# First modulation by column groups on TensorE, another last norm, and another instruction order up to the first FFN

## The chip, the core and the metric

One core of one Trainium2 chip runs the program, with its matrix engine (TensorE, PE in the profile), its vector engine (VectorE, DVE), its scalar engine (ScalarE, ACT), GpSimd (POOL) and SyncE (SP), which issues most DMAs. The metric is the device time of one execution, in microseconds, as the median over the runs.

## The reference

Two DeepNorm layers on a sequence of 512 positions of width 1024, all in float32. Each layer has a mixer and a SwiGLU channel mixer, and each of these four sublayers is modulated by the conditioning vector `c`:

```python
def ada_modulation(c, w, b):
    m = jax.nn.silu(c) @ w + b
    shift, scale, gate = jnp.split(m[:, None, :], 3, axis=-1)
    return shift, scale, gate

def residual_update(x, c, ada_w, ada_b, ln_g, ln_b, sublayer):
    shift, scale, gate = ada_modulation(c, ada_w, ada_b)
    out = sublayer(x * (1 + scale) + shift)
    return layer_norm(ALPHA * x + (1 + gate) * out, ln_g, ln_b)

def layer_norm(x, g, b):
    mu = jnp.mean(xf, axis=-1, keepdims=True)
    var = jnp.mean(jnp.square(xf - mu), axis=-1, keepdims=True)
    y = (xf - mu) * lax.rsqrt(var + LN_EPS)
    return y * g + b
```

`w` is 1024 x 3072 for each sublayer. Layer 0 mixes with sparse attention beside a chunked gMLP after one combined input projection; layer 1 with a short gated convolution. Nothing of `x * (1 + scale) + shift` can be multiplied by the first input projection before the first shift and scale are there.

## The kernel before

The 512 positions are four tiles of 128 rows (`t` = 0 to 3), the width eight chunks of 128 (`k` = 0 to 7). A float32 product is made of three products of rounded halves: high x high, high x low and low x high, each a matmul of 128 x 128 weights and 512 moving columns. So every weight is cast once (`hi`, ScalarE) and subtracted once (`lo`, VectorE or GpSimd), and every activation too.

*The start.* The chunks come in groups, `groups_k` = (0), (1), (2,3), (4,5), (6), (7). For each group SyncE loads, in this order, two slabs of modulation weights `aw` (shift and scale, `w` = 0 and 1; `group_load`, L777), the group's columns of `x` (`x_load`, L781) and the rows of three units of input weights (`unit_load`, L796). The modulation of a group is a sum over 1024 products: `ada_add` (L330, L332) multiplies each slab's column of eight by a scalar of silu(c) and adds on VectorE into `acs`, and `group_mms` (L824) adds over the partitions by a product with ones into `pq`. For slab (0, 0) alone (`ON_PE`) TensorE makes the whole sum, in eight products of one column. `group_sum` adds the bias. Then `x_turn` (L839) transposes the chunk into `px`, `x_affine` (L844) applies scale and shift into `v`, `x_high` (L850) casts it to `h`, `x_low` makes the low half, and `first_mms` (L861, L864) multiplies it with three units into six accumulators. ScalarE casts the weights of the units (`unit_high`, L803) in between. When the first unit's accumulators are complete, ScalarE copies them to `G` (L995), and the compression of keys (L1025, `pc`) reads `G`.

*Later modulations* are loaded as slabs `ar` and `ad` (L1099). Some are added on VectorE; others already by column groups on TensorE: `add` (L1108) puts 32 columns of `cz`, which are zero but for one column of silu(c), as weights into one of four column groups of the array, with 256 moving columns of the slab. `ad` has one buffer.

*The order.* `Plan` holds tasks, each with engines that it may run on, costs, dependencies and ring buffers. A plan isn't solved when the kernel is built: `Plan.follow` emits the tasks in the order of a table of numbers, `ORDER_0` and `ORDER_1`, where a number is four times the task's index plus the chosen engine. `ORDER_0` covers the start, `ORDER_1` everything from there up to the first four tiles of the first FFN. Each engine and each DMA queue does its work in the order of emission. Everything after that is written in program order, the same in both kernels but for the last norm.

*The end.* `tail_norm` (L1806) makes the last output product tile by tile; `Norm.rstd` and the function `newton` (L633) find 1/sqrt(var + eps) by an integer first guess and three Newton steps; `Norm.store` (L578) applies it. In the last norm (`s` = 3) the steps of tiles 0 to 2 run on ScalarE, nine small operations, then ScalarE scales (L585) and GpSimd multiplies and adds the rows of weights (L586, L587). For tile 3 VectorE does the steps and, in pieces of 512, 256 and 256 columns, the rest (L591, L593).

Of the kernel before, what the change touches and what calls it, by code (L numbers as in the profile page):

```python
# [7 lines left out]
F32 = mybir.dt.float32  # L8
# [214 lines left out]
def trunk(ctx: ExitStack, tc: tile.TileContext, x, c, ada_w, ada_b, ln_g, ln_b, even_w_in,  # L223
# [1582 lines left out]
    def tail_norm(acts, us, norm):  # L1806
# [3 lines left out]
        for t in range(ST):  # L1810
# [22 lines left out]
            if norm.s == 3:  # L1833
                norm.store(t, *pend)
# [195 lines left out]
```

## Time and profile before

| what | value |
|---|---|
| three runs | 1242.0, 1243.58 (median), 1244.14 us |
| the profiled execution | 1241.4 us, its span 1239.5 us |
| mean granted TensorE clock of it | 0.995 of full |
| busy: TensorE, VectorE, ScalarE, GpSimd | 1197.7, 781.1, 445.3, 137.4 us |

The span is what the profile covers of one execution; the 1.9 us between it and the execution's time lie around it. A timeline row has a start, a length, the operation with out and in by the program's names, and in brackets the idle time before and what ended it. Matmuls follow each other in a pipeline, so the step from one start to the next tells their rate better than their length does. The granted clock of 1.00 is 2.4 GHz.

### The profile page before, as it was taken

What the parts mean: (1) busy time and instruction counts of PE and PEld (TensorE: products, weight loads), DVE (VectorE), ACT (ScalarE), POOL (GpSimd) and SP (SyncE); (2) the same over time, 40 slices, a digit from 0 to 9 for tenths busy, and PEclk for the clock granted to TensorE, in tenths of its full rate; (3) what the DMA queues carried; (4) which work ended last, traced back from release to release, by engine and by line L of the source; (5) the groups of instructions that cost most, each with busy time, mean ns of one, the idle gap of its engine ahead of it and who ended that gap; (6) DMA issues with size and microseconds to landing.
All of it is one profiled execution on the core that took longest, in us unless ns stands there. A gap on an engine that the chain in (4) does not pass through costs nothing.

```text
span 1239.5 us, 15445 instructions
## 1 busy us (share of the span) xinstructions
PE 1197.7 (97%) x5939; PEld 981.9 (79%) x5939; DVE 781.1 (63%) x1306; ACT 445.3 (36%) x776; POOL 137.4 (11%) x235
## 2 busy tenths in 40 slices
PE   5899999998999999999999999999999999999996
PEld 4777777767988888888887988788988888888885
DVE  4775567886667675757766688456674353435346
ACT  2373258895423131212224422124423131313124
POOL 3130013475000000000002000002010000000005
PEclk9899999999999999999999999999999999999998
DMA  9784652131366455555630366330363232423301
GB/s 297 216 273 153 201 173 75 46 120 52 105 219 201 138 188 162 169 179 187 194 112 1 103 204 221 99 105 1 102 204 102 65 108 67 136 68 103 102 1 68
DMA packets 121465, 164.73 MB, mean 133 GB/s; under 512 B 5861, under 2 KB 87085, under 8 KB 121392
## 3 DMA queue, kind: packets, MB, share of 16 engines
q1 hardware_dynamic: 105552, 132.33, 34.0%
q10 hardware_dynamic: 14208, 26.75, 6.6%
q0 software_dynamic: 1632, 4.67, 1.3%
q8 instruction: 46, 0.75, 0.2%
q14 instruction: 27, 0.22, 0.1%
HBM read 161.63 MB, written 2.10 MB: 132 GB/s over the span
## 4 chain that ended last, share of the span: by engine, by line
PE 91%; DVE 3%; DMA 2%; ACT 2%; issue 1%; POOL 0%; SPq 0%; ACTq 0%; DVEq 0%
PE pi L524 51%; PE po L536 25%; PE pi L1269 5%; PE pi L861 1%; PE ph L1458 1%; DMA ar<-in_ada_w_dram 1%; PE po L1108 1%; PE ptp L1625 1%; PE pt L660 1%; PE pc L1025 1%; PE pi L864 1%; PE pvo L1639 1%; PE pvo L1640 1%; DMA ad<-in_ada_w_dram 0%; DMA aw<-in_ada_w_dram 0%
## 5 line engine op out<-in xcount | busy, mean ns | idle before, releaser
L524 PE MATMUL pi<-h,hi 128*128 128x512 f32 (+1 forms) x2016 | 576.0, 371 | 0.0
L524 PEld LDWEIGHTS pi<-h,hi 128*128 128x128 f32 x2016 | 365.2, 188 | 66.2 <-issue 1.4
L524 PE MATMUL pi<-h,lo 128*128 128x512 f32 (+1 forms) x1008 | 372.8, 370 | 0.0
L472 ACT ACTIVATE hi<-raw 128x1024 fp32r<-128x1024 f32 (+1 forms) x186 | 187.2, 1045 | 279.6 <-PE po L536 141.8
L476 DVE TENSOR_TENSOR lo<-raw,hi 128x1024 fp32r<-128x1024 f32 (+1 forms) x178 | 211.0, 1225 | 84.3 <-ACT hi L472 82.7
L524 PEld LDWEIGHTS pi<-h,lo 128*128 128x128 f32 x1008 | 189.7, 188 | 33.0
L541 DVE TENSOR_TENSOR xr<-xr,po 128x512 f32<-128x512 f32 x129 | 87.1, 681 | 128.5 <-PE po L536 128.3
L536 PE MATMUL po<-hi,ah 128*128 128x512 f32 (+1 forms) x420 | 165.8, 395 | 0.2
L536 PE MATMUL po<-hi,al 128*128 128x512 f32 (+1 forms) x420 | 164.5, 392 | 0.0
L536 PE MATMUL po<-lo,ah 128*128 128x512 f32 (+1 forms) x420 | 164.3, 391 | 0.0
L536 PEld LDWEIGHTS po<-hi,ah 128*128 128x128 f32 x420 | 79.0, 188 | 19.9 <-DVE xr L541 1.9
L536 PEld LDWEIGHTS po<-lo,ah 128*128 128x128 f32 x420 | 79.1, 188 | 17.7 <-issue 0.2
L536 PEld LDWEIGHTS po<-hi,al 128*128 128x128 f32 x420 | 79.0, 188 | 17.8
L1881 ACT ACTIVATE ah<-sg 128x512 fp32r<-128x512 f32 x44 | 27.8, 632 | 173.5 <-DVE sg L1926 173.5
L1926 DVE TENSOR_TENSOR sg<-sg,pi 128x512 f32<-128x512 f32 x44 | 30.2, 687 | 90.5 <-PE pi L524 90.3
L462 DVE TENSOR_TENSOR raw<-raw,gateb 128x1024 f32<-128x1024 f32 x60 | 70.9, 1219 | 4.1 <-DMA raw<-in_even_w_out_dram 4.1
L1922 ACT ACTIVATE sg<-pi 128x512 f32<-128x512 f32 x44 | 26.2, 595 | 117.3 <-PE pi L524 117.2
L332 DVE SCALAR_TENSOR_TENSOR acc<-ar,cs,acc 128x512 f32<-128x512 f32 x84 | 63.0, 750 | 3.3 <-DMA ar<-in_ada_w_dram 1.5
L1269 PE MATMUL pi<-hi,h 128*128 128x512 f32 (+1 forms) x192 | 59.8, 377 | 0.0
L1882 DVE TENSOR_TENSOR al<-sg,ah 128x512 fp32r<-128x512 f32 x44 | 30.5, 693 | 30.7 <-ACT ah L1881 30.7
L670 ACT ACTIVATE v<-pt,b,g 128x128 f32<-128x128 f32 x88 | 32.9, 454 | 44.0 <-PE pt L660 35.7
L637 POOL TENSOR_SCALAR v<-mv 128x1 f32<-128x1 f32 x10 | 2.5, 254 | 394.8 <-DVE mv L572 394.6
(255 smaller groups left out, 1250.3 us busy)
## 6 DMA issues: line engine op xcount, KB each, us to landing
raw<-in_ffn_w_in_dram SPq DMA_DIRECT2D x88, 512.0 KB, 4.6
ar<-in_ada_w_dram ACTq DMA_DIRECT2D x48, 512.0 KB, 4.3
raw<-in_ffn_w_out_dram SPq DMA_DIRECT2D x44, 512.0 KB, 4.3
ar<-in_ada_w_dram SPq DMA_DIRECT2D x24, 512.0 KB, 5.5
raw<-in_odd_w_in_dram SPq DMA_DIRECT2D x24, 512.0 KB, 4.6
raw<-in_even_w_in_dram SPq DMA_DIRECT2D x10, 512.0 KB, 5.3
aw<-in_ada_w_dram SPq DMA_DIRECT2D x8, 512.0 KB, 6.0
aw<-in_ada_w_dram SPq DMA_DIRECT2D x4, 1024.0 KB, 8.9
```

Of the source, the lines that this page charges most:

```text
L332: dve.scalar_tensor_tensor(acc, r, cs[:, k:k + 1], acc, op0=ALU.mult, op1=ALU.add)
L462: e.tensor_tensor(z[:, k, :], z[:, k, :], gateb[fold == 2], op=ALU.mult)
L472: act(hl[0][:, i * n0:i * n0 + n0], raw(i), AF.Copy)
L476: e.tensor_tensor(hl[1][:, sl], self.raw.pop(2 * u + i), hl[0][:, sl], op=ALU.subtract)
L524: mm(p[:, sl], w, h[z][k // 4][:, k % 4, sl], start=k == 0 and i == 0, stop=k == KT - 1 and i == 2)
L536: mm(p[:, c], s_, w[:, k % 2, c0], start=first and i == 0, stop=last and i == n - 1)
L541: dve.tensor_tensor(z, z, p[:, c], op=ALU.add)
L670: act(v[:, q, :], p[:, q, :], AF.Identity, scale=g1[s][:, k:k + 1], bias=b1[s][:, k:k + 1])
L1269: mm(tiles[t], s_, w[:, q, :], start=k == 0 and z == 0, stop=k == 7 and z == 2)
L1881: act(a[0][:, k, :], f, AF.Copy)
L1882: dve.tensor_tensor(a[1][:, k, :], f, a[0][:, k, :], op=ALU.subtract)
L1926: dve.tensor_tensor(f, f, p, op=ALU.mult)
```

## The change

*Start.* `ON_PE` now lists all six groups. `group_cols` makes, for each group and `w`, eight products with the four column groups (`tile_position`), with the same `cz` weights as the later modulations; `group_settle` copies the result `pg` to `acs` on ScalarE; `group_mms` adds over the partitions with ones, now always one product for a chunk. VectorE's `ada_add` isn't used for these groups.

```diff
-    def group_mms(g, w, on_pe):
+    def group_cols(g, w):
+
+        n = len(groups_k[g]) * P
+        if w == 0:
+            bx["pa", g] = ps.tile([P, 2, n], F32, name="pg", tag="tr")
+        for i in range(2):
+            for q in range(4):
+                k = 4 * i + q
+                mm(bx["pa", g][32 * q:32 * q + 32, w, :], cz[:, k // 2, k % 2:k % 2 + 32],
+                   bx["aw", g, w][:, k, :], start=i == 0, stop=i == 1,
+                   tile_position=(0, 32 * q))
+
+    def group_settle(g):
+        n = len(groups_k[g]) * P
+        bx["acc", g] = st.tile([P, 2, n], F32, name="acs", bufs=2)
+        act(bx["acc", g], bx["pa", g], AF.Copy)
+
+    def group_mms(g, w):
         n = len(groups_k[g])
         if ("pm", g) not in bx:
             bx["pm", g] = ps.tile([P, 2, n], F32, name="pq", tag="tr")
         for j in range(n):
-            sl = slice(j * P, j * P + P)
-            for k in range(KT) if on_pe else (0,):
-                mm(bx["pm", g][:, w, j:j + 1],
-                   bx["aw", g, w][:, k, sl] if on_pe else bx["acc", g][:, w, sl],
-                   cs[:, k:k + 1] if on_pe else ones[:, 0:1], start=k == 0,
-                   stop=not on_pe or k == KT - 1)
+            mm(bx["pm", g][:, w, j:j + 1], bx["acc", g][:, w, j * P:j * P + P], ones[:, 0:1],
+               start=True, stop=True)
...
-    ON_PE = ((0, 0),)
+    ON_PE = (0, 1, 2, 3, 4, 5)
...
+        if g in ON_PE:
+            got = []
+            for w in (0, 1):
+                got.append(plan.add(("pe", .1 + .28 * n, lambda g=g, w=w: group_cols(g, w)),
+                                    [aws[g][w][1], cz_t] + got[-1:], k0, acq=[] if w else ["tr"]))
+            head = last = plan.add(("act", .12 + .21 * n, lambda g=g: group_settle(g)), got, k0,
+                                   acq=["acc"], rel=[(got[0], "tr")])
```

*Planner.* The cost of an addition on TensorE is lower, and the Newton steps of the first layer's norms may run on GpSimd or VectorE.

```diff
-            last = plan.add(("pe", .5, lambda i=i: add(i)), [a, last], key,
+            last = plan.add(("pe", .3, lambda i=i: add(i)), [a, last], key,
...
-        nt = plan.add(("pool", 2.9, lambda: mid.update(n=norm.newton(mid["mv"]))), [a], key)
+        nt = plan.add([("pool", 3.3, lambda: mid.update(n=norm.newton(mid["mv"]))),
+                       ("dve", 2.3, lambda: mid.update(n=norm.newton(mid["mv"], dve)))], [a], key)
```

*Order.* Both tables are new; the first rows of `ORDER_0`:

```diff
-0 484 1104 12 4 28 40 52 64 8 16 76 88 100 112 20 32 124 136 36 44 508 148 48 56 160 60 68 172 72
...
+0 496 484 1108 12 4 28 40 52 64 44 8 76 16 48 88 100 112 124 20 32 136 148 36 56 524 160 60 68 500
```

What that moves, by place (numbers behind the names are the compiler's buffers).

TensorE from the program's start to its first input products, before (`pq` is the sum, `px` the transposed chunk, `pi` an accumulator of the first products):

```order
L824 MATMUL pq_156<-cs_96,aw_135 128x1 x8
L303 MATMUL pt_177<-ident_82,prow_98 128x19 x8
L824 MATMUL pq_156<-ones_81,acs_171 128x1
L839 MATMUL px_225<-ident_82,xr_95 128x128 x4
L861 MATMUL pi_129<-h_125,hi_192 128x512
L864 MATMUL pi_129<-h_125,lo_193 128x512
L861 MATMUL pi_130<-h_125,hi_192 128x512
L864 MATMUL pi_130<-h_125,lo_193 128x512
L861 MATMUL pi_129<-h_126,hi_192 128x512
```

and now (`pg` takes the column-group products):

```order
L837 MATMUL pg_161<-aw_133,cz0_107 32x128 x8
L837 MATMUL pg_161<-aw_135,cz0_107 32x128 x8
L301 MATMUL pt_184<-ident_82,prow_96 128x19 x8
L851 MATMUL pq_197<-ones_81,acs_193 128x1 x2
L864 MATMUL px_215<-ident_82,xr_93 128x128 x4
L837 MATMUL pg_229<-aw_145,cz0_107 32x128 x8
L886 MATMUL pi_129<-h_123,hi_199 128x512
L889 MATMUL pi_129<-h_123,lo_200 128x512
L886 MATMUL pi_130<-h_123,hi_199 128x512
L889 MATMUL pi_130<-h_123,lo_200 128x512
L837 MATMUL pg_229<-aw_147,cz0_107 32x128 x8
L886 MATMUL pi_127<-h_123,hi_156 128x512
```

The first groups' column products come first and are then mixed into the stream of first products; the sums with ones read what ScalarE copied.

ScalarE at the same place, before (`hi` is a cast weight, `v` and `h` the modulated chunk):

```order
L294 ACTIVATE cz0_109<-cs_96 128x4 x2
L803 ACTIVATE hi_192<-raw_140 128x256
L305 ACTIVATE pc_101<-pt_177 128x152
L803 ACTIVATE hi_198<-raw_142 128x256
L803 ACTIVATE hi_203<-raw_145 128x256
L803 ACTIVATE hi_198<-raw_142 128x256
L803 ACTIVATE hi_192<-raw_140 128x256
L803 ACTIVATE hi_203<-raw_145 128x256
L844 ACTIVATE v_236<-px_225,b1_0_121,g1_0_117 128x512
L850 ACTIVATE h_125<-v_236 128x512
```

and now:

```order
L815 ACTIVATE hi_156<-raw_138 128x256
L844 ACTIVATE acs_193<-pg_161 128x256
L815 ACTIVATE hi_199<-raw_140 128x256
L303 ACTIVATE pc_99<-pt_184 128x152
L815 ACTIVATE hi_207<-raw_143 128x256
L869 ACTIVATE v_224<-px_215,b1_0_119,g1_0_115 128x512
L875 ACTIVATE h_123<-v_224 128x512
L844 ACTIVATE acs_264<-pg_229 128x256
L815 ACTIVATE hi_156<-raw_138 128x256
L815 ACTIVATE hi_199<-raw_140 128x256
```

The first chunk's `v` and `h` stood behind the casts of the second group's weights; now they stand ahead of them, behind the first `acs`.

SyncE's last loads before the first FFN, before (`ad` and `gb` are modulation weights and bias, `raw` the FFN's weights):

```order
L443 DMA raw_2478<-in_ffn_w_in_dram 128x4x256
L443 DMA raw_2506<-in_ffn_w_in_dram 128x4x256
L1099 DMA ad_2634<-in_ada_w_dram 128x2x512
L443 DMA raw_2638<-in_ffn_w_in_dram 128x4x256
L443 DMA raw_2675<-in_ffn_w_in_dram 128x4x256
L1099 DMA ad_2752<-in_ada_w_dram 128x2x512
L443 DMA raw_2794<-in_ffn_w_in_dram 128x4x256
L443 DMA raw_2852<-in_ffn_w_in_dram 128x4x256
L1099 DMA ad_2857<-in_ada_w_dram 128x2x512
L443 DMA raw_3257<-in_ffn_w_out_dram 128x1024
L443 DMA raw_3260<-in_ffn_w_out_dram 128x1024
```

and now:

```order
L441 DMA raw_2496<-in_ffn_w_in_dram 128x4x256
L1122 DMA gb_2607<-in_ada_b_dram 128x512
L1127 DMA ad_2624<-in_ada_w_dram 128x2x512
L441 DMA raw_2761<-in_ffn_w_in_dram 128x4x256
L441 DMA raw_2796<-in_ffn_w_in_dram 128x4x256
L1127 DMA ad_2842<-in_ada_w_dram 128x2x512
L1127 DMA ad_2957<-in_ada_w_dram 128x2x512
L1127 DMA ad_3049<-in_ada_w_dram 128x2x512
L441 DMA raw_3268<-in_ffn_w_out_dram 128x1024
L441 DMA raw_3271<-in_ffn_w_out_dram 128x1024
```

Two `raw` loads stood between any two of the last `ad` loads; now the last three `ad` loads follow each other.

*The last norm.* `store` finds the root by VectorE's reciprocal and ScalarE's square root, with one Newton step behind it on VectorE; for tile 3 the first 512 columns are centred between the two. `tail_norm` issues a square root of a flag ahead of its tiles, so that ScalarE's table is loaded there.

```diff
+            mv = self.aggr(t)
             z = xr[:, t, :]
...
+            dve.tensor_scalar(v, mv[:, 1:2], EPS, None, op0=ALU.add)
+            dve.reciprocal(v, v)
+            act(y, v, AF.Sqrt)
+            dve.tensor_scalar(hv, mv[:, 1:2], EPS, 0.5, op0=ALU.add, op1=ALU.mult)
+
+            def center(c):
+                dve.scalar_tensor_tensor(z[:, c], z[:, c], mv[:, 0:1], self.rowg[:, c],
+                                         op0=ALU.subtract, op1=ALU.mult)
...
+            def root():
+                dve.tensor_scalar(q, y, y[:, 0:1], hv[:, 0:1], op0=ALU.mult, op1=ALU.mult)
+                dve.tensor_scalar(y, q, 1.5, y[:, 0:1], op0=ALU.subtract, op1=ALU.mult)
+
             if t < 3:
                 nb = vp.tile([P, 1], F32, name="nb", tag="nb", bufs=2)
-                act(nb, mv[:, 0:1], AF.Identity, scale=y[:, 0:1])
+                root()
+                dve.tensor_scalar(nb, mv[:, 0:1], y[:, 0:1], -1.0, op0=ALU.mult, op1=ALU.mult)
...
+            for i, c in enumerate((slice(0, 512), slice(512, 768), slice(768, D))):
+                center(c)
+                if i == 0:
+                    root()
+                scale(c)
                 nc.scalar.dma_start(out[0, t * P:(t + 1) * P, c], z[:, c])
...
+        if norm.s == 3:
+
+            act(vp.tile([P, 1], F32, name="y", tag="ny", bufs=2), flag, AF.Sqrt)
```

The form of `newton` for ScalarE and its constant `less` go. `rstd` calls `newton` for the other norms as before.

## Rows read from the trace of the kernel before

**Rows 1.** The page, busy time of each engine, its share and instructions.

```profile
PE 1197.7 (97%) x5939; PEld 981.9 (79%) x5939; DVE 781.1 (63%) x1306; ACT 445.3 (36%) x776; POOL 137.4 (11%) x235
```

**Rows 2.** Windows, core 0: stretch, length, busy time by engine, clock, DMA share, GB/s.

```profile
20.00:40.00 20.00, 14.70 (x67) 11.72 (x67) 17.96 (x52) 7.24 (x12) 0.62 (x2) 0.87 1.11 322
240.00:260.00 20.00, 15.71 (x92) 12.17 (x91) 18.00 (x64) 19.93 (x52) 12.88 (x15) 1.00 0.44 145
280.00:300.00 20.00, 16.26 (x87) 12.28 (x86) 12.53 (x22) 11.69 (x29) 10.16 (x23) 1.00 0.24 79
```

**Rows 3.** TensorE's waits, 60 to 310: line waited, releaser, total, times, longest.

```profile
PE aa L1108 <- DMA ad<-in_ada_w_dram: 2.1, 1, 2.1
...
PE pvo L1612 <- DVE mixf L1670: 1.5, 2, 1.3
```

**Rows 4.** TensorE's timeline, first 70 us: start, us, operation, [idle before, releaser].

```profile
11.28 1.09 PE L839 MATMUL px<-ident,xr 128*128 128x128 f32 x4
17.91 0.80 PE L861 MATMUL pi<-h,hi 128*128 128x512 f32 x1 [5.54 <-ACT h L850]
...
18.93 0.63 PE L861 MATMUL pi<-h,hi 128*128 128x512 f32 x1
19.36 0.63 PE L864 MATMUL pi<-h,lo 128*128 128x512 f32 x1
...
36.59 0.80 PE L861 MATMUL pi<-h,hi 128*128 128x512 f32 x1 [2.42 <-ACT h L850]
...
41.72 0.39 PE L861 MATMUL pi<-h,hi 128*128 128x512 f32 x1
41.95 0.39 PE L864 MATMUL pi<-h,lo 128*128 128x512 f32 x1
...
68.97 1.30 PE L1025 MATMUL pc<-G,w 128*128 128x64 f32 x10 [1.67 <-ACT G L995]
```

**Rows 5.** ScalarE's timeline, 8 to 20 us.

```profile
15.50 1.03 ACT L803 ACTIVATE hi<-raw 128x256 fp32r<-128x256 f32 x3 [4.33 <-DMA raw<-in_even_w_in_dram]
16.43 0.76 ACT L844 ACTIVATE v<-px,b,g 128x512 f32<-128x512 f32 x1
```

**Rows 6.** Groups by line, VectorE's L332: count, busy us, mean ns, idle before.

```profile
L332 DVE SCALAR_TENSOR_TENSOR acc<-ar,cs,acc 128x512 f32<-128x512 f32 x84 | 63.0, 750 | 3.3 <-DMA ar<-in_ada_w_dram 1.5
...
L332 DVE SCALAR_TENSOR_TENSOR acs<-aw,cs,acs 128x128 f32<-128x128 f32 (+1 forms) x77 | 26.4, 403 | 0.2
```

**Rows 7.** TensorE's timeline at two places with column-group matmuls, L1108.

```profile
83.81 1.07 PE L1108 MATMUL po<-ar,cz 128*32 128x256 f32 x16
84.81 0.88 PE L1025 MATMUL pc<-G,w 128*128 128x64 f32 x6
...
115.08 0.39 PE L1269 MATMUL pi<-hi,h 128*128 128x512 f32 x1
115.40 0.64 PE L1108 MATMUL po<-ar,cz 128*32 128x256 f32 x8
...
116.31 0.39 PE L1269 MATMUL pi<-lo,h 128*128 128x512 f32 x1
```

**Rows 8.** VectorE's timeline at the end.

```profile
1229.13 0.15 DVE L637 TENSOR_SCALAR v<-mv 128x1 f32<-128x1 f32 x1
...
1231.14 0.99 DVE L591 SCALAR_TENSOR_TENSOR xr<-xr,mv,rowg 128x512 f32<-128x512 f32 x1
1232.17 1.63 DVE L593 SCALAR_TENSOR_TENSOR xr<-xr,y,rowb 128x512 f32<-128x512 f32 x1
1233.72 1.48 DVE L591 SCALAR_TENSOR_TENSOR xr<-xr,mv,rowg 128x256 f32<-128x256 f32 x1
```

**Rows 9.** ScalarE's timeline at the end.

```profile
1224.53 0.29 ACT L643 ACTIVATE q<-y 128x1 f32<-128x1 f32 x1 [0.60 <-DVE y L639]
...
1228.09 1.52 ACT L585 ACTIVATE xr<-xr,nb,y 128x512 f32<-128x512 f32 x2
```

**Rows 10.** GpSimd's timeline at the end.

```profile
1233.33 1.59 POOL L587 TENSOR_TENSOR xr<-xr,rowb 128x512 f32<-128x512 f32 x1
```

More of the change, by code (lines that the diff above doesn't have):

```diff
@@ L246, in trunk @@
     flag = const.tile([P, 1], F32, name="flag")
-    less = const.tile([P, 1], F32, name="less")
     sel = const.tile([P, 2], F32, name="sel")
     pool.memset(ones, 1.0)
-    pool.memset(less, -1.5)
     pool.affine_select(ident, ones, pattern=[[-1, P]], base=0, channel_multiplier=1,
@@ L575, in rstd, with store, scale @@
         def rstd(self, t):
-            return self.newton(self.aggr(t), dve if t == 3 else pool if self.s < 3 else nc.scalar)
-        def store(self, t, mv, y):
+            return self.newton(self.aggr(t), dve if t == 3 else pool)
+        def store(self, t):
+            mv = self.aggr(t)
             z = xr[:, t, :]
+            v = vp.tile([P, 1], F32, name="v", tag="nv", bufs=2)
+            hv = vp.tile([P, 1], F32, name="hv", tag="nh", bufs=2)
+            y = vp.tile([P, 1], F32, name="y", tag="ny", bufs=2)
+            q = vp.tile([P, 1], F32, name="q", tag="nq", bufs=2)
+            dve.tensor_scalar(v, mv[:, 1:2], EPS, None, op0=ALU.add)
[5 more added lines that the diff above has]
+                                         op0=ALU.subtract, op1=ALU.mult)
+            def scale(c):
+                dve.scalar_tensor_tensor(z[:, c], z[:, c], y[:, 0:1], self.rowb[:, c],
+                                         op0=ALU.mult, op1=ALU.add)
+            def root():
+                dve.tensor_scalar(q, y, y[:, 0:1], hv[:, 0:1], op0=ALU.mult, op1=ALU.mult)
+                dve.tensor_scalar(y, q, 1.5, y[:, 0:1], op0=ALU.subtract, op1=ALU.mult)
             if t < 3:
                 nb = vp.tile([P, 1], F32, name="nb", tag="nb", bufs=2)
-                act(nb, mv[:, 0:1], AF.Identity, scale=y[:, 0:1])
+                root()
+                dve.tensor_scalar(nb, mv[:, 0:1], y[:, 0:1], -1.0, op0=ALU.mult, op1=ALU.mult)
                 for c in (slice(512, D), slice(0, 512)):
@@ L589, in store @@
                 return
-            for c in (slice(0, 512), slice(512, 768), slice(768, D)):
-                dve.scalar_tensor_tensor(z[:, c], z[:, c], mv[:, 0:1], self.rowg[:, c],
-                                         op0=ALU.subtract, op1=ALU.mult)
-                dve.scalar_tensor_tensor(z[:, c], z[:, c], y[:, 0:1], self.rowb[:, c],
-                                         op0=ALU.mult, op1=ALU.add)
+            for i, c in enumerate((slice(0, 512), slice(512, 768), slice(768, D))):
[3 more added lines that the diff above has]
+                scale(c)
                 nc.scalar.dma_start(out[0, t * P:(t + 1) * P, c], z[:, c])
@@ L633, in newton @@
     def newton(e, var, v, hv, y, q):
-        on_act = e is nc.scalar
-        f = dve if on_act else e
-        f.tensor_scalar(v, var, EPS, None, op0=ALU.add)
-        f.tensor_scalar(hv, var, EPS, 0.5, op0=ALU.add, op1=ALU.mult)
-        f.tensor_scalar(y.bitcast(I32), v.bitcast(I32), -0.5, float(0x5f3759df),
+        e.tensor_scalar(v, var, EPS, None, op0=ALU.add)
+        e.tensor_scalar(hv, var, EPS, 0.5, op0=ALU.add, op1=ALU.mult)
+        e.tensor_scalar(y.bitcast(I32), v.bitcast(I32), -0.5, float(0x5f3759df),
                         op0=ALU.mult, op1=ALU.add)
         for _ in range(3):
-            if on_act:
-                act(q, y, AF.Identity, scale=y[:, 0:1])
-                act(q, q, AF.Identity, scale=hv[:, 0:1], bias=less[:, 0:1])
-                act(y, y, AF.Identity, scale=q[:, 0:1])
-            else:
-                e.tensor_scalar(q, y, y[:, 0:1], hv[:, 0:1], op0=ALU.mult, op1=ALU.mult)
-                e.tensor_scalar(y, q, 1.5, y[:, 0:1], op0=ALU.subtract, op1=ALU.mult)
+            e.tensor_scalar(q, y, y[:, 0:1], hv[:, 0:1], op0=ALU.mult, op1=ALU.mult)
+            e.tensor_scalar(y, q, 1.5, y[:, 0:1], op0=ALU.subtract, op1=ALU.mult)
     def new_h():
@@ L891, in trunk @@
     h_t = {}, {}
+    cz_t = plan.add((None, 5.5, None), (), -100)
     for g, ks_ in enumerate(groups_k):
@@ L894, in trunk @@
         k0 = -100 + 7.5 * ks_[0]
-        tn = own = None
-        head, last = None, {}
-        on_dve = [w for w in (0, 1) if (g, w) not in ON_PE]
-        for ks in ((0, 1, 2), (3, 4, 5), (6, 7)) if on_dve else ():
-            z = plan.add(("dve", (.12 + .17 * n) * len(ks) * len(on_dve),
-                          lambda g=g, ks=ks, on_dve=on_dve: group_add(g, on_dve, ks), 1),
-                         [last.get(1)] + [aws[g][w][1] for w in on_dve], k0,
-                         acq=["acc"] if ks[0] == 0 else [])
-            head, last = head or z, {w: z for w in on_dve}
-        for w in (0, 1):
-            on_pe = w not in on_dve
-            tn = plan.add(("pe", n * (1.75 if on_pe else .25),
-                           lambda g=g, w=w, on_pe=on_pe: group_mms(g, w, on_pe)),
-                          [tn, last.get(w), aws[g][w][1]], k0, acq=[] if w else ["tr"],
-                          rel=[(head, "acc")] if w and head else [])
+        tn = own = head = last = None
+        if g in ON_PE:
[5 more added lines that the diff above has]
+                                   acq=["acc"], rel=[(got[0], "tr")])
+        for ks in ((0, 1, 2), (3, 4, 5), (6, 7)) if g not in ON_PE else ():
+            last = plan.add(("dve", (.12 + .17 * n) * len(ks) * 2,
+                             lambda g=g, ks=ks: group_add(g, (0, 1), ks), 1),
+                            [last] + [aws[g][w][1] for w in (0, 1)], k0,
+                            acq=["acc"] if ks[0] == 0 else [])
+            head = head or last
+        for w in (0, 1):
+            tn = plan.add(("pe", n * .25, lambda g=g, w=w: group_mms(g, w)), [tn, last], k0,
+                          acq=[] if w else ["tr"], rel=[(head, "acc")] if w else [])
             own = own or tn
@@ L1831, in tail_norm @@
                     norm.low()
-            pend = norm.rstd(t)
             if norm.s == 3:
-                norm.store(t, *pend)
+                norm.store(t)
+            else:
+                pend = norm.rstd(t)
             if t == 2 and ws.ready < min(us[-1] + 3, len(ws.units)):
```

2 lines of the change are left out of this document (removed), and 150 rows, old and new, of tables (ORDER_0, ORDER_1).

## Prediction

> **What bounds the kernel now.** I read the page first, then the table by windows, then TensorE's waits between the start and the first FFN, then the timelines of both ends. The page: TensorE is busy for 1197.7 of 1239.5 us [rows 1]. A change that leaves its matrix products as they are can win only what lies in the 41.8 us between, or what a lower clock costs. The windows tell where that is. Of those I list, 20 to 40 us has TensorE busy for 14.70, so idle for 5.30, at a mean granted clock of 0.87; 240 to 260 is idle for 4.29 and 280 to 300 for 3.74, both at full clock [rows 2]. The longest single wait after the start is 2.1 us, for a load of modulation weights (`ad`) [rows 3]. The rest is the first 18 us, where nothing can be multiplied yet, and the end.
>
> The start, in TensorE's timeline [rows 4]: the first of 144 `first_mms` products begins at 17.91, after 5.54 us of waiting for ScalarE's `h`. From there to the wait that ends at 68.97 (1.67 us, for ScalarE's `G`, so the work ends at 67.30) it is one stream. Products first follow each other at 0.43 us (18.93, 19.36), later at 0.23 (41.72, 41.95): these are the levels of 1.2 and 2.4 GHz. Seven products from 17.91 and eleven from 36.59 are at the lower level, each time after an idle stretch (5.54 and 2.42 us); the second time it is over by 41.72. Eighteen by 0.20 is 3.6 us lost.
>
> Why 17.91? The row ahead of it is not VectorE's but ScalarE's: `v` of the first chunk starts at 16.43, right behind three weight casts that waited 4.33 us for a DMA and ran from 15.50 [rows 5]. Engines keep their order, so `v` sat behind casts of the next chunk.
>
> **The change part by part.** *Accumulation moved to TensorE.* VectorE loses 77 multiply-adds, 26.4 us in all [rows 6], and 11 first multiplies. VectorE isn't what TensorE waits for longest in this stretch; what this buys is room. TensorE gains twelve blocks of eight column-group matmuls and sixteen small products with ones, of which the old code had fifteen (the eight-step sum for the first chunk goes). Two blocks run before anything could be multiplied and one more while it waits for `h`; nine lie inside the stream.
>
> Their price: the same form, 32 columns of `cz` as weights and a moving tile of 256 columns, is there in the later additions. One addition of four such products in the code is eight matmuls in the profile, so a block of eight products is sixteen, and sixteen of 256 columns hold the engine from 83.81 to 84.81, 1.00 us [rows 7]. In a place with products on both sides the step from 115.08 to 116.31 is 1.23 us, where two products and eight matmuls make 0.23 + 0.50 + 0.23 = 0.96: 0.27 for going into the column groups and out [rows 7]. The four blocks with 256 moving columns so cost 1.27 each, 5.1. For the five with 128 no row exists: 0.77 if time goes by columns, 1.27 if it goes by matmuls. I take 0.85, near the first, since the plain products too take about their columns' time; 4.2. Together 9.3.
>
> The Trainium skill speaks against such blocks: TensorEngine Tiling (Array Packing), Key Properties, says that a change of tiling mode drains TensorE, so each block breaks the stream twice. The row's 0.27 us agrees and is 2.4 of my 9.3 us; a kernel without that rule's drain would come out 2.4 us earlier than my sum.
>
> *The new order at the start.* In ScalarE's new list `v` and `h` of the first chunk stand ahead of all casts of the second. The transposes were done at 12.37 in the old run (11.28 + 1.09 [rows 4]), so `v` can begin 4.0 earlier than 16.43, and the first product comes at about 13.9 instead of 17.91. The stream in the old run is 67.30 - 17.91 = 49.4 us; less 5.3 idle [rows 2] and 3.6 at the lower clock it is 40.5 of work. New: 13.9 + 40.5 + 9.3 blocks, + 1.8 for one slow stretch instead of two, + 1.0 idle left = 66.5. The old wait of 1.67 for `G` I count as covered: in the new list some 24 products, 5.5 us, stand between the last product of the first unit, whose evacuation makes `G`, and the compression. So the compression starts at 66.5 instead of 68.97: **-2.5**. Ends: all nine blocks at 1.27 (+2.1), the slow clock as before (+1.8) and the wait for `G` still there (+1.2) make +2.6; blocks at 1.00 and 0.50, as if the change of groups were hidden (6.5 in all, so 2.8 less), make -5.3.
>
> *The new order from 60 to 310.* The wait of 2.1 [rows 3] has a reason in SyncE's list: pairs of weight loads stand between the last `ad` loads, and a pair waits for its buffer first. In the new list the last three `ad` loads stand together, and the last of the adds has moved into the first FFN tiles, with some 27 products, 6 us, between two adds. I take that wait as gone (2.1). The other idle time of 240 to 300 is 4.29 + 3.74 - 2.1 = 5.9 us; it has many owners, the next of them VectorE's `mixf` with 1.5 us in two waits [rows 3]. An order can remove some of these and make others: I take a third, 1.9. **-4.0**. Ends: nearly all of the 8.0 gone, -8; new waits of twice what is removed, +4.
>
> *The last norm.* For tile 3 the old chain is nine steps from 1229.13 to 1231.14, 0.22 each, then the first 512 columns by `L591` from 1231.14 and `L593` from 1232.17 [rows 8]. New: three small steps, two polishing steps, and the root on ScalarE under the first centring: four steps fewer ahead of `L593`, 0.9, so about 1.0 with what the root leaves free. For tiles 0 to 2 ScalarE's nine steps and `nb` (1224.53 to 1228.09, 3.6 us) [rows 9] become one root and six steps on VectorE (1.3), so GpSimd's chain, which ends at 1233.33 + 1.59 [rows 10], can start and end up to 2 us earlier. That matters for VectorE: beside GpSimd `L591` and `L593` take 0.99 and 1.63, and 1.48 at 256 columns, where the same form at 512 columns takes a mean 0.75 elsewhere [rows 6]. That is 0.2, 0.9 and over 0.7, some 2 us lost, of which I give 1.3 back. The new small steps delay VectorE's next evacuation by up to 0.5 us, of which I count 0.3. Together **-2.0**. Ends: everything lost to GpSimd given back, -3.0; nothing of it, and the delay whole, -0.5. The table load for the root stands at the start of the stage, where ScalarE has pauses; without that cover it would cost its own length once.
>
> The Trainium skill has a rule on this too: SBUF — State Buffer, Who interferes with whom, says that only the port pair shared by VectorE and GpSimd contends, as an exclusive lock. By that the centring, moved forward into GpSimd's time, would only shift the wait, and the tail would be worth its lower end, -0.5, and the sum 1.5 less.
>
> **Sum.** -2.5 - 4.0 - 2.0 = -8.5 on the profiled execution's 1241.4, so 1232.9. The median of the runs, 1243.58, lies 2.2 above that execution; about **1235** for the new median. Within 0.2%, or 2.5 us, I call it the same: about what a measurement of this kernel can tell.
>
> **Rivals.** *A, the order wins nearly all.* Middle term -8 instead of -4, tail -3: 1230. For: the head groups and the tiles of the output projection don't depend on each other, so there are products to put ahead of a late one. Against: from 240 to 260 ScalarE is busy for 19.93 of 20 [rows 2], so no order hides what waits for it there. *B, the order gives half and the blocks are dear.* Nine blocks at 1.27 leave 0.4 of the start's gain, the middle is worth 2.0, the tail 1.0: 3.4 below the old median, 1240. For: each of the old waits may come back elsewhere when the work is moved. *C, slower: TensorE stays at 1.2 GHz.* In the old run the lower clock came with work after idle time. The new stream is broken by column blocks and starts earlier against the same loads, so pauses between chunks are likely. Were the clock low from 13.9 to 36, sixty products at 0.20 are 12 us and five blocks at 0.77 more another 4, less the 1.8 assumed: +14, which makes 1246 to 1249 by what the middle gives. From some fifty slow products on (the 1.8 and the 8.5 of the sum, at 0.20) it is slower than before. Against: in the old run the level rose after seven and after eleven [rows 4]. *D, it does nothing:* the start's gain ends at the first later load, since the loads keep their order there, and new waits make up for the old; 1243.6.
>
> **How the numbers follow.** The forecast, 1231 to 1239, has 0.55; A 0.15, B 0.17, C 0.08, D 0.05. The range 1228 to 1242 takes in the first three, and leaves out C, D and the far ends. Faster is the forecast, A and most of B (0.05 of its 0.17 lies within 2.5 us of the old median): 0.82; the same, that 0.05 and D: 0.10; slower, C: 0.08.
>
> **What would show it.** In the new profile: the first product at 13 to 15 us; blocks of eight in the stream with gaps from product to product of 0.8 to 1.5 us over the usual 0.23; the compression before 68; no wait of over 1 us for `ad`; idle time of 240 to 300 near 4 instead of 8; GpSimd's last step ending 4 to 5 us after VectorE's first step behind the last aggregate, where it was 5.8 before (1234.92 against 1229.13 [rows 8, 10]). I am wrong in the start if the compression comes after 70, wrong in the middle if the idle time there is 7 or more, and wrong in the tail if the time from VectorE's last evacuation to the end is not at least 0.5 us shorter.

## The result, and the profile after

The changed kernel takes 1236.62 us (median of four runs, 1233.65 to 1237.01) against 1243.13 for the kernel before (1242.0 to 1244.14): a ratio of 0.9943, 95% interval 0.9925 to 0.9961. That is faster by 6.5 us, and beyond 0.2%. Timed again later it took 1235.42 against 1242.79, ratio 0.9945 [0.9932, 0.9959]. The profiled execution has a span of 1231.7 us, 7.8 less than the one of before; it is the shortest of the four, and another profile of the same code has 1234.0. So the pair of profiles shows up to 1.3 us more gain than the medians.

The page, busy time by engine (to compare with [rows 1]):

```profile
PE 1206.0 (98%) x6117; PEld 983.2 (80%) x6117; DVE 752.4 (61%) x1213; ACT 442.3 (36%) x760; POOL 136.4 (11%) x239
```

TensorE is busy 8.3 us longer and idle 16.1 us less. The windows (columns as in [rows 2]):

```profile
20.00:40.00 20.00, 19.01 (x135) 12.73 (x134) 4.49 (x10) 6.67 (x11) 2.14 (x5) 1.00 1.10 319
240.00:260.00 20.00, 15.67 (x80) 12.60 (x80) 17.03 (x68) 18.90 (x55) 13.48 (x10) 0.91 0.52 168
280.00:300.00 20.00, 19.20 (x122) 14.56 (x121) 16.50 (x35) 11.67 (x27) 10.26 (x24) 1.00 0.17 53
...
245.00:250.00 5.00, 5.00 (x24) 4.36 (x23) 4.05 (x12) 4.77 (x13) 3.23 (x3) 0.71 0.67 224
```

From 20 to 40 us idle time fell from 5.30 to 0.99, from 280 to 300 from 3.74 to 0.80. From 240 to 260 it stayed at 4.33, and now at a granted clock of 0.91: in 245 to 250 it is 0.71. TensorE's waits from 55 to 310 us, the two longest (to compare with [rows 3]):

```profile
PE pvo L1668 <- DVE pr L1662: 2.5, 2, 2.3
PE pvo L1667 <- ACT pr L1658: 1.8, 2, 1.6
```

The wait for `ad` is gone, and so is that for `mixf`. Two new ones, 1.6 and 2.3 us, stand in their place.

TensorE's timeline at the start (to compare with [rows 4]):

```profile
13.63 0.80 PE L886 MATMUL pi<-h,hi 128*128 128x512 f32 x1 [0.48 <-ACT h L875]
14.23 0.63 PE L889 MATMUL pi<-h,lo 128*128 128x512 f32 x1
14.65 0.63 PE L886 MATMUL pi<-h,hi 128*128 128x512 f32 x1
...
15.64 1.08 PE L837 MATMUL pg<-aw,cz 128*32 128x128 f32 x16
...
22.46 0.61 PE L886 MATMUL pi<-h,hi 128*128 128x512 f32 x2
23.00 1.07 PE L837 MATMUL pg<-aw,cz 128*32 128x256 f32 x16
...
24.34 0.40 PE L889 MATMUL pi<-h,lo 128*128 128x512 f32 x1
...
46.26 0.63 PE L886 MATMUL pi<-h,hi 128*128 128x512 f32 x2
46.82 0.64 PE L837 MATMUL pg<-aw,cz 128*32 128x128 f32 x16
...
47.73 0.39 PE L889 MATMUL pi<-h,lo 128*128 128x512 f32 x1
...
65.83 3.68 PE L1053 MATMUL pc<-G,w 128*128 128x64 f32 x32
```

The first product begins at 13.63 instead of 17.91. The compression begins at 65.83 instead of 68.97, with no wait. From 22.46 to 24.34 lie three products and a block of 256 columns: 1.88 - 0.69 = 1.19 for the block. From 46.26 to 47.73 lie three and a block of 128 columns: 1.47 - 0.69 = 0.78. ScalarE (to compare with [rows 5]) starts `v` at once when the transposes are done, since no cast stands ahead of it:

```profile
12.14 0.78 ACT L869 ACTIVATE v<-px,b,g 128x512 f32<-128x512 f32 x1 [1.30 <-PE px L864]
```

The end, on VectorE, ScalarE and GpSimd (to compare with [rows 8 to 10]):

```profile
1223.27 0.15 DVE L584 TENSOR_SCALAR v<-mv 128x1 f32<-128x1 f32 x1
...
1223.59 1.36 DVE L590 SCALAR_TENSOR_TENSOR xr<-xr,mv,rowg 128x512 f32<-128x512 f32 x1
...
1225.42 1.20 DVE L594 SCALAR_TENSOR_TENSOR xr<-xr,y,rowb 128x512 f32<-128x512 f32 x1
1226.54 0.47 DVE L590 SCALAR_TENSOR_TENSOR xr<-xr,mv,rowg 128x256 f32<-128x256 f32 x1
```

```profile
1200.82 1.28 ACT L1841 ACT_TABLE_LOAD   x1
...
1223.14 1.26 POOL L607 TENSOR_TENSOR xr<-xr,rowg 128x512 f32<-128x512 f32 x1
1224.48 1.59 POOL L608 TENSOR_TENSOR xr<-xr,rowb 128x512 f32<-128x512 f32 x1
```

From VectorE's first step behind the last aggregate to `scale` of 512 columns it is 2.15 us, 3.04 before. GpSimd ends 2.8 us after that first step, 5.8 before, so the 256-column centring takes 0.47 instead of 1.48. Two more GpSimd rows of before belong to this comparison:

```profile
1230.32 1.26 POOL L587 TENSOR_TENSOR xr<-xr,rowb 128x512 f32<-128x512 f32 x1
1231.54 1.71 POOL L586 TENSOR_TENSOR xr<-xr,rowg 128x512 f32<-128x512 f32 x1
```

Each of these VectorE steps reads `xr` and a row of weights, and one that begins while a GpSimd step runs ends a fixed time behind the end of that GpSimd step. For 512 columns it is 0.55 us in all four cases: 1232.13 behind 1231.58 and 1233.80 behind 1233.25 before, 1224.95 behind 1224.40 and 1226.62 behind 1226.07 now. For 256 columns it is 0.28, 1235.20 behind 1234.92. So three steps were held up before, and two are now. The same times stand in the other twelve traces, to 0.01 us. The table for the root is loaded at 1200.82, while ScalarE has nothing else to do.

### The profile page after: what moved, and what is told of

Its sections match the earlier page's. It is cut to its first block, busy times and chain, and to the rows that moved or that the text cites. A ratio compares the mean times of both kernels' runs of the same rounds, so it can differ in the third digit from the quotient of the medians.

```text
span 1231.7 us, 15693 instructions
## 1 busy us (share of the span) xinstructions
PE 1206.0 (98%) x6117; PEld 983.2 (80%) x6117; DVE 752.4 (61%) x1213; ACT 442.3 (36%) x760; POOL 136.4 (11%) x239
## 4 chain that ended last, share of the span: by engine, by line
PE 94%; DVE 2%; ACT 2%; POOL 1%; issue 1%; DMA 0%; ACTq 0%; POOLq 0%
PE pi L522 51%; PE po L534 25%; PE pi L1297 5%; PE pi L886 1%; PE ptp L1653 1%; PE po L1136 1%; PE ph L1486 1%; PE pt L672 1%; PE pi L889 1%; PE pvo L1668 1%; PE po L886 1%; PE pvo L1667 1%; PE pg L837 1%; PE pc L1053 1%; ACT sc L1565 1%
## 5 line engine op out<-in xcount | busy, mean ns | idle before, releaser
L474 DVE TENSOR_TENSOR lo<-raw,hi 128x1024 fp32r<-128x1024 f32 (+1 forms) x180 | 214.3, 1230 | 81.5 <-ACT hi L470 79.6
```

The lines of the kernel that those rows point to most:

```text
L474: e.tensor_tensor(hl[1][:, sl], self.raw.pop(2 * u + i), hl[0][:, sl], op=ALU.subtract)
```

## The experiments

The parts were undone and done alone, then the two causes that the trace suggests were tried one by one.

**The last norm undone.** The functions `store`, `newton` and `tail_norm` are those of before.

```diff
-            return self.newton(self.aggr(t), dve if t == 3 else pool)
+            return self.newton(self.aggr(t), dve if t == 3 else pool if self.s < 3 else nc.scalar)
...
-            act(y, v, AF.Sqrt)
```

> The changed kernel with the old last norm (Newton steps on ScalarE for tiles 0 to 2, on VectorE for tile 3), all else as changed. Theory, the three parts add: from the end of TensorE's last product to the end of the span the traces show 11.67 us before and 9.65 in the changed kernel, so this kernel loses 2.0 us of the changed one's gain: ratio to the kernel before about 0.996, compression still at 65.8, that last stretch again 11.5 to 11.8. Rival, the centring that is moved forward only shifts the wait for GpSimd, and the gain of the end came from elsewhere: 0.5 us or less is lost and the last stretch stays below 10.5.

1238.49 us, ratio 0.9965 [0.9953, 0.9977], so 1.9 to 3.1 us over the changed kernel's two medians. The stretch behind TensorE's last product is the long one again (table below), by 2.7 us instead of the 2.0 expected. The theory holds, its size is larger. The compression is at 67.79, not at 65.8; what that mark varies with stands below the table.

**The second order undone.** `ORDER_1` as before in the changed kernel.

> The changed kernel with the old second table of order, from the first input projection to the first FFN; start and last norm as changed. Theory: the second order is worth 2.6 us (what is left of 7.8 after 3.1 at the start and 2.0 at the end), so this one is 2 to 3.5 us slower than the changed kernel, the wait of about 2 us for the last modulation loads is back, and idle time in the stretch of 237 to 297 us is near 8 us. Rival, the second order is worth nothing or less, because its two long waits and the low clock after them cost what it saves, and the start's gain only shows late: within 1 us of the changed kernel.

1240.33 us, ratio 0.9974 [0.9963, 0.9985]: 3.7 to 4.9 over the changed kernel. The wait for `ad` is back with 2.0 us, and the idle time of 237 to 297 is 7.5. The theory holds; its size was too small, by up to 1.4 us.

**The second order alone.** `ORDER_1` as changed in the kernel before.

> The kernel before with only the new second table of order (and VectorE's form of one Newton step that it asks for). Theory: 2 to 3.5 us faster than before, with the waits for pr of 1.6 and 2.3 us, the lower clock behind them, and no wait of over 1 us for the modulation loads. Rival, the order only fits behind the new start: the waits shift or grow, and it is within 1 us of before or slower.

1241.18 us, ratio 0.9991 [0.998, 1.0002]: a gain of 2.2 us by medians and 1.1 by the ratio, and not clear of none. The waits are as the theory says; the time does not decide between theory and rival. In this trace the clock is low in two places:

```profile
20.00:40.00 20.00, 14.71 (x66) 11.61 (x66) 17.27 (x51) 7.24 (x12) 0.59 (x2) 0.90 1.11 323
240.00:260.00 20.00, 16.05 (x79) 13.16 (x78) 15.87 (x48) 18.26 (x44) 12.55 (x9) 0.83 0.49 157
```

**The start alone.** The column groups and `ORDER_0` in the kernel before.

> The kernel before with only the new start (column groups for the first modulation and the new first table of order). Theory: compression starts at 65.5 to 66.5 instead of 68.97, and the whole is 2.5 to 3.5 us faster than before. Rival, what the start wins is lost at the first later load or wait, since loads keep their order: compression at 66, but the first FFN begins less than 1 us earlier than before.

1242.53 us, ratio 0.9995 [0.9985, 1.0005]. The compression is at 67.71, so 1.3 earlier than in the trace of before, and the whole not measurably faster. The theory's 65.5 to 66.5 and its 2.5 to 3.5 us are both missed, and the time is as the rival has it. But its trace has a clock of 0.83 from 240 to 260, where the trace of before, with the same code in that stretch, has 1.00 [rows 2]:

```profile
240.00:260.00 20.00, 17.52 (x88) 14.13 (x89) 16.72 (x57) 18.98 (x48) 12.26 (x14) 0.83 0.46 145
```

0.17 of 20 us is 3.4 us, an estimate of what it costs there. Low stretches of this kind come and go between executions with the same code at that place, and one trace against another can't tell a part's worth. So I set the stages of seven traces side by side. Marks are the start of the compression, of the output projection's last product, of TensorE's last product, and the span's end; each column is the time from one mark to the next.

| kernel | start to compression | to the last of the projection | to TensorE's last | to the end |
|---|---|---|---|---|
| before | 68.97 | 233.92 | 924.66 | 11.95 |
| second order alone | 69.95 | 231.74 | 925.64 | 12.37 |
| start alone | 67.71 | 235.74 | 924.76 | 11.99 |
| last norm undone | 67.79 | 231.29 | 925.61 | 12.61 |
| second order undone | 67.24 | 237.41 | 924.80 | 9.65 |
| changed | 65.83 | 230.33 | 925.61 | 9.93 |
| changed, again | 67.86 | 230.53 | 925.66 | 9.95 |

By means of the kernels that have a part and those that don't: start 67.29 against 69.46, -2.2; second order 230.97 against 235.69, -4.7, with +0.9 given back later, where the last addition now lies among the FFN's products; last norm 9.84 against 12.23, -2.4. Together -8.4. The second and third parts differ from trace to trace by less than these means; the first does not. The changed start stands unedited in two more traces, those of the two edits at 240 us below, with the compression at 66.22 and 69.68. With them the mean is 67.5, the part is worth -2.0, and seven traces of one start lie 3.9 us apart. They differ above all in how long TensorE keeps the lower pace: four products go at 0.43 us at the start of the trace with 66.22, eight in the changed kernel's first, and fifteen in the one with 69.68, which is slow again from 34.07 on. So the size of the start's gain is known to about 2 us only.

**`v` behind the casts again.** Nine numbers of `ORDER_0` are moved (a part of the table).

```diff
-268 552 280 108 116 556 564 292 120 128 304 132 140
+268 116 120 128 132 140 144 588 596 604 552 280 108 556 564 292 304
```

> The changed kernel with nine numbers of its first table moved, so that ScalarE's v and h of the first chunk stand behind the three weight casts of the second group again, as before. Theory, the first product was late for that reason: it comes at 17 to 18 us instead of 13.6, and the compression 2 to 4 us later than in the changed start (65.8 to 67.8 in four traces), so 69 to 71. Rival, the start is bound by when later groups' loads land: compression stays within 1 us of 67, and idle time of TensorE between 25 and 40 us shrinks by what the first product lost.

```profile
17.79 0.80 PE L888 MATMUL pi<-h,hi 128*128 128x512 f32 x1 [4.18 <-ACT h L877]
```

First product at 17.79, compression at 69.87; 1238.77 us, ratio 0.9963 [0.9951, 0.9975], so about 2 to 3 us slower than the changed kernel. The theory holds. The mark alone would not show it, since 69.68 occurs with the changed start too. But this trace has the same eight products at 0.43 us and the same clock of 1.00 from 20 to 40 as the changed kernel's first, and its first product is 4.2 us later, its compression 4.0. ScalarE's order at this one place is worth as much as the whole start.

**The two new waits.** In the trace of the changed kernel, TensorE's list, then ScalarE's and VectorE's:

```profile
241.61 0.51 PE L1667 MATMUL pvo<-pr,vpk 128*128 128x512 f32 x1 [1.61 <-ACT pr L1658]
244.38 0.72 PE L1668 MATMUL pvo<-pr,vpk 128*128 128x512 f32 x1 [2.27 <-DVE pr L1662]
244.89 0.63 PE L1667 MATMUL pvo<-pr,vpk 128*128 128x512 f32 x1
```

```profile
237.18 3.89 ACT L470 ACTIVATE hi<-raw 128x1024 fp32r<-128x1024 f32 x4
...
241.44 1.36 DVE L474 TENSOR_TENSOR lo<-raw,hi 128x1024 fp32r<-128x1024 f32 x1
242.73 0.68 DVE L1662 TENSOR_TENSOR pr<-ptp,pr 128x512 fp32r<-128x512 f32 x1
```

`pr`, which TensorE waits for, stands behind four weight casts of 1024 columns (3.89 us) on ScalarE and a weight's low half (1.36) on VectorE. Behind the wait the products start 0.43 us and more apart. So first the order (two of the four moved numbers are in this part of the table):

```diff
-4344 3756 4325 2748 2764 4376 2780 2796 2768
+4344 3756 4325 2748 2764 3744 4376 2780 2796 3748 2768
```

> The changed kernel with four numbers of its second table moved: of the four weight casts of 1024 columns that ScalarE does from 237 to 241 us, two go behind the casts of pr, and VectorE's lows of pr go ahead of a weight's low. Theory, the waits of 1.6 and 2.3 us at 240 to 244 are ScalarE's and VectorE's order alone: both go below 0.6, the granted clock of 240 to 260 is 1.00 instead of 0.83 to 0.91, and the kernel is 2 to 5 us faster than the changed one. Rival, the two engines are full there (18.9 and 17.0 of 20 us): the wait comes back at a later product of the same stretch, idle time of 237 to 265 stays over 3.5 us, and the time is within 1 us.

```profile
251.55 0.49 PE L1667 MATMUL pvo<-pr,vpk 128*128 128x512 f32 x1 [2.27 <-ACT pr L1658]
```

1236.4 us, ratio 0.994 [0.9928, 0.9951]: the same. The waits at the old place are gone (0.43 the longest), but one of 2.27 us for ScalarE's `pr` has come at 251.55, products at 0.43 us follow it, and the clock of 240 to 260 is 0.91 again. The rival holds. ScalarE is busy here for 18.60 of 20 us, as [rows 2] had it with 19.93, and this order only placed the wait elsewhere. Whether another order can do without it was not tried.

Then the pause itself, filled:

```diff
             mm(un.o, w, pairs[x][0], start=False, stop=False)
+            for _ in range(8 if (i, g, x) == (2, 1, 2) else 0):
+                mm(un.o, w, pairs[x][0], start=False, stop=False)
```

> The changed kernel with eight more products in TensorE's list right ahead of the product that waits 2.3 us at 242; they repeat the product before it into the same sum, so one unit's attention is not the reference's. They take 8 x 0.23 = 1.8 us at full clock and so fit into the wait. Theory, the low clock behind the wait comes from TensorE's pause: the granted clock of 240 to 260 is 1.00, and the kernel is 1.5 to 3 us faster than the changed one though it does more. Rival, the low clock comes there whatever TensorE did: clock 0.83 to 0.91 as before, products at 0.43 us behind the wait, the same time or up to 1 us slower.

```profile
245.89 2.02 PE L1669 MATMUL pvo<-pr,vpk 128*128 128x512 f32 x8
248.32 0.50 PE L1670 MATMUL pvo<-pr,vpk 128*128 128x512 f32 x1 [0.41 <-DVE pr L1662]
248.66 0.39 PE L1667 MATMUL pvo<-pr,vpk 128*128 128x512 f32 x1
248.89 0.39 PE L1670 MATMUL pvo<-pr,vpk 128*128 128x512 f32 x1
```

(All of it is some 4 us later than in the changed kernel's trace; this is the one with the compression at 69.68.) The wait falls to 0.41, the products behind it follow at 0.23, and the granted clock of 240 to 260 is 1.00. One trace would not settle this, but all of them together do. With the new order and the pauses left open the clock there is 0.83 or 0.91 in every one of seven traces; with one or both pauses filled it is 1.00 in all four (this one and the last three below). So the low clock there came from TensorE's pause. With the old order, whose longest pause there is 1.3 us, it is 1.00 once (before) and 0.83 twice. The time, 1235.41 us, ratio 0.9936 [0.9925, 0.9948], is 1.2 below the first median and the same as the second: the mechanism is shown, the gain is not.

**The first products.** All eight from 13.63 on start 0.43 apart, or further, though the clock that the profile gives is 1.00 there.

```diff
+    def warm(n):
+        for _ in range(n):
+            mm(first[0], hot[:, 0:P], hot, start=True, stop=True)
```

> The changed kernel with twelve products of 512 columns that no result reads, in TensorE's list where it waits for the first loads: seven ahead of the first column groups, two, two and one in the gaps up to the first product. Theory, the first eight products go at 0.43 us because TensorE did only narrow work and paused before them: now they follow at 0.23, the first block among them takes 0.6 instead of 1.0, and the compression is 1.5 to 2.5 us earlier than in the changed start, 63.5 to 66. Rival, the pace of the first products doesn't depend on what went before, or the loads set the pace from 25 us on: first products at 0.43, compression at 66 to 68, or later by what the added products delay.

```profile
13.75 0.63 PE L898 MATMUL pi<-h,hi 128*128 128x512 f32 x1
14.18 0.63 PE L901 MATMUL pi<-h,lo 128*128 128x512 f32 x1
...
15.59 0.66 PE L847 MATMUL pg<-aw,cz 128*32 128x128 f32 x16
16.18 0.50 PE L898 MATMUL pi<-h,hi 128*128 128x512 f32 x1
16.51 0.39 PE L901 MATMUL pi<-h,lo 128*128 128x512 f32 x1
16.75 0.40 PE L898 MATMUL pi<-h,hi 128*128 128x512 f32 x1
```

Half a success: four products at 0.43, the block behind them in 0.59 and the others at the fast pace; compression at 64.86, earlier than in any of the seven traces without these products. 1235.02 us, ratio 0.9934 [0.9921, 0.9947], which is not clear of the changed kernel's. In this trace the recorded clock of 12 to 20 us is 0.79.

**Both together, output whole.** The fill multiplies by a broadcast zero, in both waits, and three more warm products stand ahead of the second group's first block.

> The changed kernel itself, unedited, on the same chip as the next one, for a tighter interval. Both theories: 1235 to 1238, ratio about 0.9945; its first eight input products at 0.43 us, and the two waits for pr at about 240 with a granted clock below 0.95 in 240 to 260.

This came as expected: 1235.42 us, some eight products at 0.43, both waits, and a clock of 0.91 over 240 to 260.

> The changed kernel with both additions to TensorE's list, and the output whole: the twelve products of the warm start and three more ahead of the second group's first block; and in the two waits of the unit at 240 six and eight products of the unit's weights with a broadcast zero, which add nothing to its sum. Theory, the two gains add (1.6 and 1.2 us by medians against the changed kernel): 1233 to 1234.5, compression at 64 to 65.5, the granted clock of 240 to 260 at 1.00, and the mean clock of the runs at 0.996 or more. Rival, the clock goes down elsewhere instead, at the next pause, or products with zeros don't count as work: mean clock 0.993 to 0.995 as in the changed kernel, and the time within 1 us of it.

```profile
13.19 0.40 PE L902 MATMUL pi<-h,hi 128*128 128x512 f32 x1
13.42 0.39 PE L905 MATMUL pi<-h,lo 128*128 128x512 f32 x1
...
27.65 1.05 PE L865 MATMUL pq<-ones,acs 128*128 128x1 f32 x8 [1.73 <-ACT acs L858]
...
30.73 0.80 PE L902 MATMUL pi<-h,hi 128*128 128x512 f32 x1 [0.99 <-ACT h L889]
31.32 0.63 PE L905 MATMUL pi<-h,lo 128*128 128x512 f32 x1
31.75 0.63 PE L902 MATMUL pi<-h,hi 128*128 128x512 f32 x1
```

1233.2 us, ratio 0.9921 [0.9908, 0.9934], 2.2 below the changed kernel on the same chip (1235.42). The first product now starts at 13.19 and the next 0.23 later. Products by zero counted as work here: 240 to 260 is at 1.00. But the compression is at 67.52, a miss: the faster stream runs into the third group, waits 1.73 for `acs`, and the clock of 20 to 40 falls to 0.83. The mean clock of the runs, 0.994 to 0.996, misses the 0.996 or more too. The rival is right that the clock goes down at another pause, and wrong on the time. On ScalarE that copy stands behind a cast that waits for a DMA, the same fault as with `v`:

```profile
26.48 0.63 ACT L815 ACTIVATE hi<-raw 128x512 fp32r<-128x512 f32 x1 [8.19 <-DMA raw<-in_even_w_in_dram]
27.02 0.58 ACT L858 ACTIVATE acs<-pg 128x512 f32<-128x512 f32 x1
```

**The copy ahead of the cast,** one number of `ORDER_0` moved (636 ahead of 668), without and with more zero products in the pauses behind it:

> The last kernel (warm start and both fills) with one number of its first table moved: ScalarE copies the third group's column sums to acs ahead of the cast of that group's weights, behind which it stood until 27.0 us because the cast waits for a DMA. Theory, the wait of 1.7 us before the products with ones goes below 0.5, the products that follow come 0.5 to 1.5 us earlier than 30.7, the granted clock of 20 to 40 stays at 0.95 or more, and compression is at 64.5 to 66.5 instead of 67.5; 1231 to 1233. Rival, the third group's own load sets that place: products again at 30 to 31, and the time within 1 us of 1233.2.

> The same, with three and four products by a broadcast zero into an open sum ahead of the products with ones and of the third group's first input product, where TensorE pauses. Theory, with no pause left the clock stays up: granted clock of 20 to 40 at 1.00, compression at 63.5 to 65.5, mean clock of the runs 0.996 or more, 1230 to 1232.5. Rival, the added products only delay what comes behind them: compression no earlier than in the kernel without them, and the time the same within 1 us.

1232.99 us [ratio 0.9922, 0.9908 to 0.9936] and 1232.43 us [0.9924, 0.9908 to 0.994]; compression at 65.51 and 65.43. Of the first, all of the theory's signs but one came: the wait for `acs` is gone, the group's products start 0.9 us earlier, at 29.80, and the compression is in its range. The clock of 20 to 40 is 0.91, though, and 1232.99 lies in the theory's range and in the rival's. The transposes now wait 0.95 us and the first product 1.09 for ScalarE's `h`; on VectorE the group's sum (27.45) stands behind a weight's low half that waited until 26.64 for a cast, and moving that was not tried. With the added zero products the rival holds: the clock is 0.91 as well, and compression and time are the same. All three versions, at 1232.4 to 1233.2, are faster than the kernel before; that they are faster than the changed one is shown on one chip for the first, and for the other two only by ratios whose intervals overlap with its own. With the fill the transposes and zero products are slow, with one input product behind them, instead of the input products:

```profile
28.09 1.74 PE L888 MATMUL px<-ident,xr 128*128 128x128 f32 x8 [0.77 <-PE pq L875]
29.48 2.05 PE L845 MATMUL pi<-naught,h 128*128 128x512 f32 x4
```

## Why the prediction was right

The time lay 1.6 us above the forecast, in its likeliest range and with its sign.

*Start, -2.5: -3.1 in the profiled pair, -2.2 by the table.* First product 13.63 (13.9 foretold), blocks 1.19 and 0.78 (1.27 and 0.85), one slow stretch of eight products instead of two, 0.99 us of idle time (1.0), no wait for `G`. Put into the prediction's sum these give 65.4 for the compression, against 65.83. The step that carried it, `v` out from behind the casts, is shown by undoing it. The single slow stretch of about eight products was luck in part: the same start had four to fifteen of them in other traces, some with a second stretch, and was worth -2.0 by all seven. The Trainium skill's drain between tiling modes (TensorEngine Tiling (Array Packing), Key Properties) is in the blocks' price as I took it from the old rows, and the price held: 1.19 is 0.19 over the 1.00 of sixteen such matmuls by themselves, where I had 0.27.

*Middle, -4.0: -2.6 in the profiled pair, -3.8 by the table.* The wait for `ad` went, as said. Of the other waits I had counted a third as gone. Those in `mixf`, `ptc` and `scc` all went, and two new ones came, 3.9 us together, where ScalarE's casts were put ahead of `pr`. So idle time in 240 to 300 fell from 8.0 to 5.3, not to 4. From 60 to 240 us, where I had counted nothing, idle time fell from 3.24 to 0.58; 1.67 of that is the wait for `G`, which belongs to the start, and some 1.0 is more gain. What I had left out is the clock behind a pause in this stretch: 0.91 over 240 to 260 is an estimated 1.8 us lost. It isn't the new order's own fault: traces with the old order have it too.

*End, -2.0: -2.0 in the profiled pair, -2.4 by the table.* Ahead of the first `scale` it is 0.89 less (0.9), in sum: the small steps gave 1.15, and the centring, now beside GpSimd for longer, took back 0.26. Less time beside GpSimd gave 1.0 on the 256-column centring and 0.4 on the `scale` before it. GpSimd's last step ends 2.8 us after VectorE's first one, sooner than the 4 to 5 foretold. The delay of 0.3 in the evacuation was not seen (1.50 from TensorE's last product to that first step, 1.58 before); 0.4 was lost behind VectorE's last step instead. While GpSimd runs, the 512-column steps still take 1.36 and 1.20, each ending 0.55 behind a GpSimd step. That agrees with the lock of the Trainium skill's SBUF — State Buffer, Who interferes with whom; but moving work into GpSimd's time didn't only shift the wait, since GpSimd ends earlier too.

*The sum.* -8.5 foretold; -7.8 for the profiled pair, -8.4 by stages, -6.5 and -7.4 by medians. Start and second order alone gained 0.8 and 2.2 by medians, and both with each other 4.8. Why they gain more together was not settled: a low clock in 240 to 260 (0.83 in both) does not explain it, since the trace with both and the old norm has 0.83 there too. Rival C fell: the lower pace lasted eight products, and fifteen and a few more in the slowest trace, not some fifty. Rival A fell on the waits for ScalarE's and VectorE's `pr` at 240 to 260, which the one other order that was tried had again; rival B on the blocks, which cost less than 1.27, and on the middle and the end, which gave more than its 2.0 and 1.0.

## What to carry to other kernels

In a list that an engine keeps to, look for the instruction that waits on a DMA and for what stands behind it: here a cast in the wrong place held the first product back by 4.2 us, and another made a wait of 1.7 us in a later version. Where an engine is all but full over a stretch, moving its work may only move the wait, as it did here. Read the worth of a part from the same stage in several traces, not from one pair of spans: one start, unedited, reached the same mark 3.9 us apart.

## What the runs showed of the hardware

The first products at the start went at 0.43 us under a granted clock of 1.00 in the profile, and products without use ahead of them brought 0.23; so the recorded clock of 1.00 doesn't tell that pace. How many products stay at 0.43 changed from four to fifteen between executions of the same start.

Pauses of 1.6 and 2.3 us, or one of 2.3 us alone, brought a granted clock of 0.83 or 0.91 over 240 to 260 in every one of the seven traces that have them, which by that share is 1.8 to 3.4 us of 20. Filled, the same place was at 1.00 in four traces of four. Pauses of at most 1.3 us at the same place brought 0.83 in two traces and 1.00 in one.

Products by zeros that add nothing kept the clock at 1.00 through the pauses at 240 us in three traces. At 28 us, where a wait of 0.77 was left beside them, they did not (0.91 over 20 to 40).

A VectorE step that reads `xr` and a row of weights and began during a GpSimd step at the end ended 0.54 to 0.56 us (512 columns) or 0.28 us (256) behind the end of that GpSimd step, in all fourteen traces. Steps that add a product `po` of TensorE to `xr` were not held: 0.68 to 0.69 us for 512 columns in the midst of GpSimd's steps.
